# Two wide products in place of three for the first token block's attention scores

## The chip, the cores and the metric

The kernel runs on one core of one Trainium2 chip, as one launch. The metric is the device time in microseconds, from launch to end; the number given for a kernel is the median of its runs. All data are float32.

## What is computed

A trunk of two layers over 512 tokens of width 2048. Both layers shift and scale their input by a condition vector, mix it with an attention, multiply by a gate and normalise:

```
mod = silu(c) @ w_mod[l] + b_mod[l]; shift, scale, gate = split(mod, 3)
h = x * (1 + scale) + shift
y = attention_l(h)
x = layer_norm(sqrt(2) * x + gate * y)
```

Layer 0 is a differential attention with 8 heads. Each head has two pairs of queries and keys (component 0 and 1, width 128) and values of width 256. Layer 1 is a "forgetting" attention with 16 heads of width 128, whose keys and values come from a projection of layer 0's output. The reference goes through the queries in blocks of 128 tokens:

```
layer 0:  sc = q_block @ k.T * 128**-0.5 - slope * (t - s);  masked where s > t
          a = softmax(sc of component 0) - lam * softmax(sc of component 1);  o = a @ v
layer 1:  sc = q_block @ k.T * 128**-0.5 + F[t] - F[s];      masked where s > t
          o = softmax(sc) @ v
```

Only keys up to the query's own token count. So the first query block needs scores against 128 keys, the second against 256, the third against 384, the fourth against 512.

## The kernel before

**Products in two halves.** TensorE multiplies in a reduced float32 form (`F32R`). To keep float32 precision the kernel splits each operand into a high half (rounded to that form by ScalarE) and a low half (what is left, by VectorE), and forms three products instead of one: high by high, high by low, low by high. The function `products` (lines 199 to 203) issues them into one accumulating PSUM bank, and every large matrix product of the kernel goes through it or through its equivalent of the opening stage. In the rows of the profile the names of a product are those of the moving operand, then of the stationary one: `sc<-kbl,qh` moves the low half of the keys past the high half of the queries.

**Stages.** The opening stage builds the modulated input while the first weights arrive; its order on each engine is written out by hand in strings (`ORDER_PE` and others). Then comes a sequence of streamed groups (`group`): weights flow through a ring of staging tiles (`wst`), are split into `whi` and `wlo` (three buffers each, lines 106 and 107) and are multiplied with the activations, kept on chip in halves (`hh`, `hl`), into four banks called `acc`. A group is 32 bursts of six products.

**Attention between the bursts.** The attention of one head (layer 0) or of a pair of heads (layer 1) is cut into small steps kept in the list `pieces`. After every burst the function `tick` takes the next one from the list. So while the weights of the next projection stream through TensorE, the attention of the head before runs in between. At the end of a group `drain` empties the list before new queries and keys are written. After the opening stage the tile framework plans the order of the instructions on each engine from modelled times; it may part products that the code issues together.

**A score step.** `score` (line 859 and following in layer 0, line 1486 and following in layer 1) takes one of two PSUM banks (`sc`), forms the score of query block `i` against the `w = (i + 1) * 128` keys it may see, adds the bias (distance and mask, or forgetting sums and mask) with one VectorE instruction that also finds the row's extreme, and lets ScalarE take the exponential. Its width on TensorE is

```
n = max(w, 256)
```

so the first block is computed against 256 keys, and only the first 128 columns are read. After the scores of a block, the probabilities are turned by a VectorE transposition and two trips through DRAM (`turn`, `send`), split into halves (`take`: `ah`, `al` in layer 0, `pTh`, `pTl` in layer 1) and multiplied with the values (`values`, bank `o`). The last head of layer 0 and the last pair of layer 1 use TensorE's transposition instead.

**Where queries and keys are kept.** In layer 0, `evac_qk` (line 823) writes q0, q1, k0 and k1 of a head out of the accumulators as separate tiles of 128 x 512 for the high and low half (`q0h`, `q0l` and so on, one buffer each). In layer 1, `split_pair` (line 1472) does this for the keys of two heads (`kbh`, `kbl`, two buffers each).

Of the kernel before, what the change touches and what calls it, by code (L numbers as in the profile page):

```python
# [11 lines left out]
F32R = mybir.dt.float32r  # L12
I32 = mybir.dt.int32
AF = mybir.ActivationFunctionType
ALU = mybir.AluOpType

P = 128
D = 2048
KT = D // P
T = 512  # L20
# [117 lines left out]
def tile_yoco(  # L138
# [24 lines left out]
    V, S, PE, G = nc.vector, nc.scalar, nc.tensor, nc.gpsimd  # L163
# [3 lines left out]
    out = out[0]  # L167
# [31 lines left out]
    def products(dst, lhs, rhs, start, stop):  # L199

        PE.matmul(dst, lhs[0], rhs[0], start=start, stop=False)  # L201
        PE.matmul(dst, lhs[0], rhs[1], start=False, stop=False)  # L202
        PE.matmul(dst, lhs[1], rhs[0], start=False, stop=stop)  # L203


    ident = const.tile([P, P], F32, name="ident")
# [616 lines left out]
    def evac_qk(h):  # L823
        def fn(b, acc):
            name = ("q0", "q1", "k0", "k1")[b]
            hi = ap.tile([P, T], F32R, name=name + "h", tag=name + "h")
            lo = ap.tile([P, T], F32R, name=name + "l", tag=name + "l")
            if b < 2:
                S.activation(hi, acc, AF.Copy, scale=QS)
                V.scalar_tensor_tensor(lo, acc, QS, hi.bitcast(F32), op0=ALU.mult, op1=ALU.subtract)  # L830
            else:
                split(hi, lo, acc)
            cur[h, name] = (hi, lo)
        return fn

    def evac_vg(h):
# [16 lines left out]
    def attention_a(h, lead=3, late=(), spread=False):  # L853
# [5 lines left out]
        def score(i, comp):  # L859
            def fn():  # L860
                if i == 0 and comp == 0:
                    bias = ap.tile([P, 512], F32, name="bias", tag="bias", bufs=1)
                    V.scalar_tensor_tensor(bias, dist, -slope, mask, op0=ALU.mult, op1=ALU.add)
                    st["bias"] = bias
                if comp == 0:
                    st["mn", i] = ap.tile([P, 2], F32, name="mn", tag="mn", bufs=2)
                    st["rs", i] = ap.tile([P, 2], F32, name="rsum", tag="rsum", bufs=2)
                w = (i + 1) * P
                n = max(w, 256)
                q, k = cur[h, f"q{comp}"], cur[h, f"k{comp}"]  # L870
                sc = sc_bank()
                ts = slice(i * P, (i + 1) * P)
                products(sc[:, :n], (q[0][:, ts], q[1][:, ts]), (k[0][:, :n], k[1][:, :n]), True, True)
                e = ap.tile([P, 512], F32, name="e", tag="e", bufs=4)
                mn, rs = st["mn", i][:, comp : comp + 1], st["rs", i][:, comp : comp + 1]
                V.tensor_tensor_reduce(  # L876
                    out=e[:, :w], in0=sc[:, :w], in1=st["bias"][:, (3 - i) * P :], scale=-1.0, scalar=3.0e38,
                    op0=ALU.add, op1=ALU.min, accum_out=mn,
                )
                S.activation(e[:, :w], e[:, :w], AF.Exp, bias=mn, scale=-1.0, accum_out=rs)  # L880
                st["e", i, comp] = e
                if comp == 1:
                    r = st["rs", i]
                    V.reciprocal(r, r)
                    V.tensor_tensor(r[:, 1:2], r[:, 1:2], neglam, op=ALU.mult)
                    e0, e1 = st["e", i, 0], e
                    V.tensor_scalar(e0[:, :w], e0[:, :w], r[:, 0:1], None, op0=ALU.mult)
                    V.scalar_tensor_tensor(e0[:, :w], e1[:, :w], r[:, 1:2], e0[:, :w], op0=ALU.mult, op1=ALU.add)
            return fn
# [582 lines left out]
    def split_pair(p):  # L1472
        vh = bp.tile([P, TB, 256], F32R, name="vbh", tag="vbh", bufs=1)
        vl = bp.tile([P, TB, 256], F32R, name="vbl", tag="vbl", bufs=1)
        split(vh, vl, cur[p, "vld"])
        cur[p, "vB"] = (vh, vl)
        for hd in (2 * p, 2 * p + 1):
            kh = bp.tile([P, T], F32R, name="kbh", tag="kbh", bufs=2)
            kl = bp.tile([P, T], F32R, name="kbl", tag="kbl", bufs=2)
            split(kh, kl, KTs[hd])  # L1480
            cur[hd, "kB"] = (kh, kl)

    def attention_b(hd):
        st = {}

        def score(i):
            def fn():
                w = (i + 1) * P
                m = max(w, 256)
                q, k = cur[hd, "q"], cur[hd, "kB"]  # L1490
                sc = sc_bank()
                ts = slice(i * P, (i + 1) * P)
                products(sc[:, :m], (q[0][:, ts], q[1][:, ts]), (k[0][:, :m], k[1][:, :m]), True, True)
                bias = bp.tile([P, 512], F32, name="biasb", tag="biasb", bufs=2)
                V.scalar_tensor_tensor(
                    bias[:, :w], cur[hd, "nf"][:, :w], F[:, i, hd : hd + 1], mask[:, (3 - i) * P :], op0=ALU.add, op1=ALU.add
                )
                e = bp.tile([P, w], F32, name="eb", tag=f"eb{i}", bufs=1)
                mn = bp.tile([P, 1], F32, name="mnb", tag="mnb", bufs=3)
                rs = bp.tile([P, 1], F32, name="rsb", tag="rsb", bufs=3)  # L1500
                V.tensor_tensor_reduce(  # L1501
                    out=e[:, :w], in0=sc[:, :w], in1=bias[:, :w], scale=-1.0, scalar=3.0e38, op0=ALU.add, op1=ALU.min, accum_out=mn
                )
                S.activation(e[:, :w], e[:, :w], AF.Exp, bias=mn, scale=-1.0, accum_out=rs)  # L1504
                V.reciprocal(rs, rs)
                V.tensor_scalar(e[:, :w], e[:, :w], rs, None, op0=ALU.mult)
                st["e", i] = e
            return fn

        def turn(i):
            def fn():
                t = bp.tile([P, (i + 1) * P], F32, name="tb", tag=f"tb{i}", bufs=1)
                V.transpose(t.rearrange("p (b j c) -> p j b c", b=4, c=32), st["e", i].rearrange("p (j b c) -> p j b c", b=4, c=32))
                st["t", i] = dram.tile([P, (i + 1) * P], F32, name="turned", tag=f"turned{i}", bufs=2)
                nc.sync.dma_start(st["t", i], t)
            return fn

        def send(i):  # L1520
            def fn():
                src = st["t", i].rearrange("(a r) (b n) -> b r a n", a=4, b=4)
                to = pTl[:, 4 * i : 4 * i + 4, 0 : i + 1, :].bitcast(F32).rearrange("p a j c -> p a (j c)")
                for b in range(4):
                    nc.sync.dma_start(to[32 * b : 32 * b + 32], src[b])
            return fn

        def take(i):
            def fn():
                hi, lo = (t[:, 4 * i : 4 * i + 4, 0 : i + 1, :] for t in (pTh, pTl))  # L1530
                S.copy(hi, lo.bitcast(F32))
                V.tensor_tensor(lo, lo.bitcast(F32), hi.bitcast(F32), op=ALU.subtract)
            return fn

        def turn_at_once(i):
            def fn():
                pt = tr_bank()
                for j in range(i + 1):
                    PE.transpose(pt[:, j * P : (j + 1) * P], st["e", i][:, j * P : (j + 1) * P], ident)
                src = pt[:, : (i + 1) * P].rearrange("p (j a c) -> p a j c", a=4, c=32)  # L1540
                hi, lo = (t[:, 4 * i : 4 * i + 4, 0 : i + 1, :] for t in (pTh, pTl))
                S.copy(hi, src)
                V.tensor_tensor(lo, src, hi.bitcast(F32), op=ALU.subtract)
            return fn

        def values(j0, j1):
            def fn():
                if j0 == 0:
                    st["o"] = o_bank()
                vh, vl = cur[hd // 2, "vB"]  # L1550
                es = slice((hd % 2) * P, (hd % 2 + 1) * P)
                for j in range(j0, j1):
                    t0 = min(j * P, 256)
                    m0 = t0 // 32
                    o = st["o"][:, t0:].rearrange("p (m c) -> p m c", c=32)
                    products(o, (vh[:, j, es], vl[:, j, es]), (pTh[:, m0:, j, :], pTl[:, m0:, j, :]), j == 0, j == 3)
                if j1 == TB:
                    ogB[hd] = ktile("ogB")
                    V.scalar_tensor_tensor(ogB[hd], st["o"], 0.5, cur[hd, "sgT"], op0=ALU.mult, op1=ALU.mult)
            return fn  # L1560

        parts = (score, turn, send, take, turn_at_once)
        return *([part(i) for i in range(TB)] for part in parts), [values(0, 2), values(2, 4)]
# [135 lines left out]
```

## Time and profile before

| | |
|---|---|
| median of 3 runs | 1944.55 us (1944.41 to 1945.12) |
| profiled execution, first to last instruction (span) | 1943.2 us |
| mean granted TensorE clock | 0.998 |
| busy: TensorE, VectorE, ScalarE | 1922.5, 1351.3, 730.3 us |
| products on TensorE | 8973 |

No time of the profiled execution is listed apart from its span, so the span is set against the median of the runs: the median is 1.35 us longer. In the rows of the timeline the first number is the start in microseconds from the beginning of the span, the second the duration in microseconds, then come engine, line, operation, and output and operands by name; in brackets stands how long the engine sat idle before it and what ended that. In the grouped rows the numbers behind the first bar are the busy time of the group in microseconds and the mean duration of one in nanoseconds; behind the second bar is the engine's idle time before them, with what ended it. Products overlap: the duration of one is its latency, and the distance between two starts is what it takes from TensorE. Layer 0's attention lies between 200 and 830 us, layer 1's between 1389 and 1790 us.

### The profile page before, as it was taken

What the parts mean: (1) busy time and instruction counts of PE and PEld (TensorE: products, weight loads), DVE (VectorE), ACT (ScalarE), POOL (GpSimd) and SP (SyncE); (2) the same over time, 40 slices, a digit from 0 to 9 for tenths busy, and PEclk for the clock granted to TensorE, in tenths of its full rate; (3) what the DMA queues carried; (4) which work ended last, traced back from release to release, by engine and by line L of the source; (5) the groups of instructions that cost most, each with busy time, mean ns of one, the idle gap of its engine ahead of it and who ended that gap; (6) DMA issues with size and microseconds to landing.
All of it is one profiled execution on the core that took longest, in us unless ns stands there. A gap on an engine that the chain in (4) does not pass through costs nothing.

```text
span 1943.2 us, 25791 instructions
## 1 busy us (share of the span) xinstructions
PE 1922.5 (99%) x8973; PEld 1619.5 (83%) x8973; DVE 1351.3 (70%) x2514; ACT 730.3 (38%) x1250; POOL 2.2 (0%) x10
## 2 busy tenths in 40 slices
PE   8999999999999999999999999999999999999997
PEld 7888888888888888888889998888888888888886
DVE  6884588777676768567675657777566666677657
ACT  3546344323332334521273222224343434353123
POOL 0000000000000000000000000000000000000000
PEclk9999999999999999999999999999999999999999
DMA  9983466676767675377557756774355555554622
GB/s 339 383 300 115 151 187 201 210 230 188 239 192 225 202 237 167 121 241 225 171 174 256 266 187 214 251 260 158 118 154 148 153 155 154 152 171 153 222 91 105
DMA packets 351630, 382.19 MB, mean 197 GB/s; under 512 B 77926, under 2 KB 260860, under 8 KB 350732
## 3 DMA queue, kind: packets, MB, share of 16 engines
q1 hardware_dynamic: 348620, 376.35, 61.6%
q10 hardware_dynamic: 2880, 4.20, 0.6%
q8 instruction: 70, 1.15, 0.2%
q14 instruction: 60, 0.49, 0.1%
HBM read 348.65 MB, written 31.80 MB: 196 GB/s over the span
## 4 chain that ended last, share of the span: by engine, by line
PE 96%; DVE 3%; DMA 1%; issue 0%; ACT 0%; SPq 0%; DVEq 0%
PE acc L201 27%; PE acc L202 27%; PE acc L203 27%; PE acc L703 4%; PE sc L703 2%; PE o L201 1%; PE o L202 1%; PE o L203 1%; PE sc L203 1%; PE sc L202 1%; PE o L703 1%; PE sc L201 1%; DVE sacc L601 1%; PE tr L643 0%; PE tr L669 0%; PE tr L629 0%
## 5 line engine op out<-in xcount | busy, mean ns | idle before, releaser
L106 ACT CAST whi<-wst 128x1024 fp32r<-128x1024 f32 (+2 forms) x298 | 303.4, 1018 | 660.7 <-PE acc L203 353.2
L107 DVE TENSOR_TENSOR wlo<-wst,whi 128x1024 fp32r<-128x1024 f32 (+2 forms) x298 | 351.4, 1180 | 261.0 <-ACT whi L106 254.5
L201 PE MATMUL acc<-hh,whi 128*128 128x512 f32 x1184 | 463.5, 391 | 0.0
L202 PE MATMUL acc<-hl,whi 128*128 128x512 f32 x1184 | 461.8, 390 | 0.0
L203 PE MATMUL acc<-hh,wlo 128*128 128x512 f32 x1184 | 460.9, 390 | 0.0
L201 PE MATMUL acc<-whi,hh 128*128 128x512 f32 (+1 forms) x1168 | 444.4, 381 | 0.0
L202 PE MATMUL acc<-wlo,hh 128*128 128x512 f32 (+1 forms) x1168 | 442.3, 379 | 0.0
L203 PE MATMUL acc<-whi,hl 128*128 128x512 f32 (+1 forms) x1168 | 441.8, 378 | 0.0
L420 DVE SCALAR_TENSOR_TENSOR macc<-ms,cact,macc 128x512 f32<-128x512 f32 x307 | 229.1, 746 | 63.1 <-DMA ms<-in_w_mod_dram 41.1
L203 PEld LDWEIGHTS acc<-hh,wlo 128*128 128x128 f32 x1184 | 222.3, 188 | 47.6
L201 PEld LDWEIGHTS acc<-hh,whi 128*128 128x128 f32 x1184 | 222.5, 188 | 43.6 <-issue 0.6
L202 PEld LDWEIGHTS acc<-hl,whi 128*128 128x128 f32 x1184 | 222.4, 188 | 42.1
L203 PEld LDWEIGHTS acc<-whi,hl 128*128 128x128 f32 x1168 | 219.2, 188 | 36.5 <-DVE hl L1280 0.2
L201 PEld LDWEIGHTS acc<-whi,hh 128*128 128x128 f32 x1168 | 219.2, 188 | 34.8 <-DVE ztmp L1194 0.4
L202 PEld LDWEIGHTS acc<-wlo,hh 128*128 128x128 f32 x1168 | 219.3, 188 | 33.6 <-DVE wlo L107 0.3
L601 DVE SCALAR_TENSOR_TENSOR sacc<-sms,cact,sacc 128x512 f32<-128x512 f32 (+1 forms) x123 | 87.5, 712 | 5.9 <-DMA sms<-in_w_mod_dram 2.6
L880 ACT ACTIVATE e<-e,mn 128x128 f32<-128x128 f32 (+3 forms) x64 | 36.0, 563 | 113.5 <-DVE mn L876 99.6
L1504 ACT ACTIVATE eb<-eb,mnb 128x128 f32<-128x128 f32 (+1 forms) x64 | 36.0, 563 | 88.0 <-DVE mnb L1501 87.8
L876 DVE CUSTOM_DVE_ANT_0 e<-sc,bias 128x128 f32<-128x128 f32 (+3 forms) x64 | 31.0, 485 | 28.1 <-PE sc L203 27.8
L125 DVE TENSOR_TENSOR wlo<-wst,whi 128x768 fp32r<-128x768 f32 (+1 forms) x32 | 34.8, 1088 | 18.7 <-ACT whi L118 9.9
L703 PE MATMUL acc<-whi,hh 128*128 128x512 f32 x128 | 46.4, 394 | 0.0
L703 PE MATMUL acc<-whi,hl 128*128 128x512 f32 x128 | 45.9, 394 | 0.0
(285 smaller groups left out, 1999.0 us busy)
## 6 DMA issues: line engine op xcount, KB each, us to landing
wst<-in_a_w_in_dram SPq DMA_DIRECT2D x240, 256.0 KB, 4.1
ms<-in_w_mod_dram SPq DMA_DIRECT2D x136, 256.0 KB, 3.7
ms<-in_kv_w_mod_dram SPq DMA_DIRECT2D x64, 512.0 KB, 4.0
wst<-in_b_w_in_dram SPq DMA_DIRECT2D x128, 256.0 KB, 3.0
sms<-in_w_mod_dram SPq DMA_DIRECT2D x56, 512.0 KB, 7.7
wst<-in_kv_w_dram SPq DMA_DIRECT2D x40, 512.0 KB, 4.2
ms<-in_w_mod_dram SPq DMA_DIRECT2D x32, 512.0 KB, 4.5
wst<-in_a_w_out_dram SPq DMA_DIRECT2D x32, 512.0 KB, 4.4
```

Of the source, the lines that this page charges most:

```text
L106: self.nc.scalar.copy(hi[:, :, :w], st[:, :, :w])
L107: self.nc.vector.tensor_tensor(lo[:, :, :w], st[:, :, :w], hi[:, :, :w].bitcast(F32), op=ALU.subtract)
L125: self.nc.vector.tensor_tensor(lo[:, :, :w], st[:, :, :w], hi[:, :, :w].bitcast(F32), op=ALU.subtract)
L201: PE.matmul(dst, lhs[0], rhs[0], start=start, stop=False)
L202: PE.matmul(dst, lhs[0], rhs[1], start=False, stop=False)
L203: PE.matmul(dst, lhs[1], rhs[0], start=False, stop=stop)
L420: ins = V.scalar_tensor_tensor(acc, w, cact[:, kt : kt + 1], acc, op0=ALU.mult, op1=ALU.add)
L601: V.scalar_tensor_tensor(acc, w, sc, acc, op0=ALU.mult, op1=ALU.add)
L703: PE.matmul(bank[n, bk], l, r, start=start, stop=stop, skip_group_check=True)
L876: V.tensor_tensor_reduce(out=e[:, :w], in0=sc[:, :w], in1=st["bias"][:, (3 - i) * P :], scale=-1.0, scalar=3.0e38, op0=ALU.add, op1=ALU.mi ...
L880: S.activation(e[:, :w], e[:, :w], AF.Exp, bias=mn, scale=-1.0, accum_out=rs)
L1504: S.activation(e[:, :w], e[:, :w], AF.Exp, bias=mn, scale=-1.0, accum_out=rs)
```

## The change

High and low halves of a query or key are placed in one tile, `[P, 2, T]`. For the first query block (`i == 0`) of both layers, the score no longer goes through `products`. The new function `corner` takes the first 128 columns of the high keys and the first 128 of the low keys as one moving operand of 2 x 128 columns, and multiplies it once with the high and once with the low half of the queries. The bank then holds, in columns 0 to 127, the products with the high keys, and in columns 128 to 255 those with the low keys (the product low by low is among them now). VectorE adds the two halves: in layer 0 the second half plus the bias is written to the unused part of the tile `e` and takes the place of the bias; in layer 1 the second half is added into the bias tile. The other three query blocks are as before.

```diff
+    def corner(sc, q, k):
+        dst, both = (t[:, :, 0:P] for t in (sc[:, 0 : 2 * P].rearrange("p (u n) -> p u n", u=2), k))
+        PE.matmul(dst, q[0], both, start=True, stop=False)
+        PE.matmul(dst, q[1], both, start=False, stop=True)
...
     def evac_qk(h):
-            hi = ap.tile([P, T], F32R, name=name + "h", tag=name + "h")
-            lo = ap.tile([P, T], F32R, name=name + "l", tag=name + "l")
+            both = ap.tile([P, 2, T], F32R, name=name, tag=name)
+            hi, lo = both[:, 0, :], both[:, 1, :]
...
+            cur[h, name, "both"] = both
...
     score, layer 0:
-                products(sc[:, :n], (q[0][:, ts], q[1][:, ts]), (k[0][:, :n], k[1][:, :n]), True, True)
+                bias = st["bias"][:, (3 - i) * P :]
+                if i:
+                    products(sc[:, :n], (q[0][:, ts], q[1][:, ts]), (k[0][:, :n], k[1][:, :n]), True, True)
+                else:
+                    corner(sc, (q[0][:, ts], q[1][:, ts]), cur[h, f"k{comp}", "both"])
+                    V.tensor_tensor(e[:, P : 2 * P], sc[:, P : 2 * P], bias, op=ALU.add)
+                    bias = e[:, P : 2 * P]
                 V.tensor_tensor_reduce(
-                    out=e[:, :w], in0=sc[:, :w], in1=st["bias"][:, (3 - i) * P :], scale=-1.0, scalar=3.0e38,
+                    out=e[:, :w], in0=sc[:, :w], in1=bias, scale=-1.0, scalar=3.0e38,
...
     split_pair, layer 1:
-            kh = bp.tile([P, T], F32R, name="kbh", tag="kbh", bufs=2)
-            kl = bp.tile([P, T], F32R, name="kbl", tag="kbl", bufs=2)
+            both = cur[hd, "kboth"] = bp.tile([P, 2, T], F32R, name="kb", tag="kb", bufs=2)
+            kh, kl = both[:, 0, :], both[:, 1, :]
...
     score, layer 1:
-                products(sc[:, :m], (q[0][:, ts], q[1][:, ts]), (k[0][:, :m], k[1][:, :m]), True, True)
+                if i:
+                    products(sc[:, :m], (q[0][:, ts], q[1][:, ts]), (k[0][:, :m], k[1][:, :m]), True, True)
+                else:
+                    corner(sc, (q[0][:, ts], q[1][:, ts]), cur[hd, "kboth"])
                 bias = ...
+                if i == 0:
+                    V.tensor_tensor(bias[:, :w], sc[:, P : 2 * P], bias[:, :w], op=ALU.add)
```

## The prediction

> **What bounds the kernel now.** I read the page first: its header, the busy times, the chain that ended last.
>
> ```profile
> span 1943.2 us, 25791 instructions
> ...
> PE 1922.5 (99%) x8973; PEld 1619.5 (83%) x8973; DVE 1351.3 (70%) x2514; ACT 730.3 (38%) x1250; POOL 2.2 (0%) x10
> ...
> PE 96%; DVE 3%; DMA 1%; issue 0%; ACT 0%; SPq 0%; DVEq 0%
> ```
>
> TensorE is busy for 1922.5 of 1943.2 us and carries 96% of the chain. A busy PE could still be a PE that waits, so the second view is the list of PE's waits; its longest entry and the only one that concerns an attention step:
>
> ```profile
> PE tr L228 <- DMA crow<-in_c_dram: 2.5, 1, 2.5
> PE o L202 <- DVE pTl L1532: 0.5, 1, 0.5
> ```
>
> The first lies at the very start. No score product (L201 to L203 into sc) is in the list with a VectorE or ScalarE wait, and no weight half. So in both attention stages a TensorE product that disappears shortens the span by its whole slot, and VectorE work is free until it makes a product late. The third view is the timeline around one first-block score of the second layer (PE alone):
>
> ```profile
> 1389.02 0.39 PE L203 MATMUL acc<-hh,wlo 128*128 128x512 f32 x1
> 1389.25 0.28 PE L201 MATMUL sc<-kbh,qh 128*128 128x256 f32 x1
> 1389.36 0.28 PE L202 MATMUL sc<-kbl,qh 128*128 128x256 f32 x1
> 1389.48 0.28 PE L203 MATMUL sc<-kbh,ql 128*128 128x256 f32 x1
> 1389.60 0.40 PE L201 MATMUL acc<-hh,whi 128*128 128x512 f32 x1
> ```
>
> The second column, 0.28 us, is the latency of a product; what it costs is the distance from its start to the next start. A product of 512 columns takes 0.23, one of 256 takes 0.11 to 0.12, and the three together 0.35 us.
>
> **The change part by part: the products.** How many scores are touched is read from the VectorE groups, shapes apart, once in the window of the first layer's attention and once in that of the second's. A first-block score is the one whose biased sum is 128 columns wide:
>
> ```profile
> L876 DVE CUSTOM_DVE_ANT_0 e<-sc,bias 128x128 f32<-128x128 f32 x16 | 4.6, 288 | 10.0 <-PE sc L203 10.0
> ```
> ```profile
> L1532 DVE TENSOR_TENSOR pTl<-pTl,pTh 128x128 fp32r<-128x128 f32 x15 | 4.4, 291 | 0.9 <-ACT pTh L1531 0.9
> L1501 DVE CUSTOM_DVE_ANT_0 eb<-sc,biasb 128x128 f32<-128x128 f32 x16 | 4.4, 272 | 6.3 <-PE sc L203 6.3
> ```
>
> 16 in the first layer (8 heads, 2 components) and 16 in the second (16 heads): 32. Each loses one product of 256 columns and its weight load. The two that stay still have 256 moving columns and still take 256 output columns, so by the rows above a corner goes from 0.35 to 0.23 or 0.24 us. The removed slot is 0.115 to 0.125 us, and 32 of them are 3.7 to 4.0 us; I take 3.8.
>
> What the trace of before does not show for a score is a moving operand in two stretches of 128 columns that lie 512 elements apart. The nearest rows are the value products of the second layer over the last two key blocks: their moving operand is cut into eight stretches of 32 columns (the tile pTh, indexed by row group and key block), which is more broken than the new one. Of six such products the first and the last:
>
> ```profile
> 1435.38 0.28 PE L201 MATMUL o<-pTh,vbh 128*128 128x256 f32 x1
> ...
> 1435.99 0.28 PE L203 MATMUL o<-pTh,vbl 128*128 128x256 f32 x1
> ```
>
> Five distances make 0.61 us, 0.122 each: no slower than the score's own by more than a few ns. The other bounds come from the spacings: a product of 512 columns costs 0.23 and two of 256 cost 0.24, so a fresh start is worth about 0.01 us. If each stretch counted as a start, a new product would cost 0.13, a corner 0.26, and the saving would be 0.09 x 32 = 2.9 us. At the other end it could be 0.11 as for the first of the three, a saving of 0.13 x 32 = 4.2 us. I take 3.8 by the value rows and keep 2.9 to 4.2. The Trainium skill has a price for this too: by its page "TensorE: Matmul & The Clock Gate", section "Back-to-back issue gap", a product of 256 columns follows the last after 256/2.4 + 2.5 = 109 ns, and by that estimate 32 slots would give 3.5 us; the rows here stand at 0.11 to 0.12, and the row decides.
>
> **VectorE's additions.** Every corner gains one addition of 128 columns, with one operand in PSUM. The three group rows above bracket it: 272 to 291 ns, whether the operand comes from sc or from SBUF; I take 0.29 us, 32 x 0.29 = 9.3 us of VectorE, of which it has 1943.2 - 1351.3 = 592 us idle. Queued behind it on VectorE are the reduction of the same score, then what follows there (reciprocals, transposes, the low halves of weights); ScalarE's exponential waits for the reduction. In the first layer the reduction sat waiting for TensorE for 10.0 us in all over its 16 corners, in the second 6.3 us, so there is room at the place itself. Two users of the result are on TensorE. One is the transposition of the last head of the first layer, which is close behind its score:
>
> ```profile
> 800.49 0.35 DVE L888 SCALAR_TENSOR_TENSOR e<-e,rsum 128x128 f32<-128x128 f32 x1
> ```
> ```profile
> 803.71 0.27 PE L897 MATMUL tr<-ident,e 128*128 128x128 f32 x1
> ```
>
> The tile is there at 800.84 and is read at 803.71: 2.9 us cover two additions of 0.29. The other is the value product of the second layer, which waits for the last split (pTl) of the first head of a pair while VectorE handles the second head's corner. An ordinary pair:
>
> ```profile
> 1401.71 0.25 DVE L1501 CUSTOM_DVE_ANT_0 eb<-sc,biasb 128x128 f32<-128x128 f32 x1
> ...
> 1404.42 0.42 DVE L1501 CUSTOM_DVE_ANT_0 eb<-sc,biasb 128x256 f32<-128x256 f32 x1 [0.45 <-PE sc L203]
> ...
> 1411.74 1.22 DVE L107 TENSOR_TENSOR wlo<-wst,whi 128x1024 fp32r<-128x1024 f32 x1
> ...
> 1414.55 0.40 PE L201 MATMUL o<-pTh,vbh 128*128 128x512 f32 x1
> 1414.69 0.65 DVE L1532 TENSOR_TENSOR pTl<-pTl,pTh 128x512 fp32r<-128x512 f32 x1
> 1414.79 0.39 PE L202 MATMUL acc<-hl,whi 128*128 128x512 f32 x1
> ...
> 1415.48 0.42 PE L202 MATMUL o<-pTl,vbh 128*128 128x512 f32 x1
> ```
>
> pTl ends at 1415.34 and is used at 1415.48: only 0.14 us to spare. But between the corner at 1401.71 and pTl, VectorE idles for 0.45 us on a product of TensorE, whose time does not move with VectorE, and that alone swallows 0.29. Cost: nothing. In the last streamed group it is different, as VectorE also splits the gated outputs (hl) there:
>
> ```profile
> 1710.70 0.16 DVE L1505 RECIPROCAL rsb<-rsb 128x1 f32<-128x1 f32 x1 [0.62 <-ACT eb L1504]
> ...
> 1712.51 0.25 DVE L1501 CUSTOM_DVE_ANT_0 eb<-sc,biasb 128x128 f32<-128x128 f32 x1
> ...
> 1720.01 0.16 DVE L1505 RECIPROCAL rsb<-rsb 128x1 f32<-128x1 f32 x1 [0.17 <-ACT eb L1504]
> ...
> 1726.36 0.65 DVE L1532 TENSOR_TENSOR pTl<-pTl,pTh 128x512 fp32r<-128x512 f32 x1
> ...
> 1727.06 0.19 PEld L202 LDWEIGHTS o<-pTl,vbh 128*128 128x128 f32 x1 [0.95 <-DVE pTl L1532]
> ```
>
> From the corner at 1712.51 to pTl the only idle time is 0.17 us, and it waits for an exponential that VectorE itself feeds, so it moves along. TensorE already waits there, and the addition makes it wait longer: 0.2 us (additions overlap their neighbours by some 0.08) to 0.29. I charge 0.25, once.
>
> **The joined tiles** (high and low half of q, k in one buffer) change no instruction's size. The first corner product now needs the low half of k, which it needed 0.11 us later before; PE's waits name no such half, so nothing. A buffer is now given back when the readers of both halves are done, 0.12 us apart; the pieces of a head are drained before its buffers are written anew, so nothing either. No DMA is added or moved.
>
> **Sum.** -3.8 + 0.25 = -3.55 us on the span of 1943.2, that is 1939.65. The median of the runs shown is 1944.55, 1.35 above that span; the same distance gives 1941.0. A measurement of this kernel can tell about 0.2%, 3.9 us, from no change: the line is at 1940.66, and the sum ends 0.3 us short of it.
>
> **The rivals.** *Placement for the better, 0.22.* The order on each engine after the opening stage is planned from modelled times, as the ordinary pair shows: the code issues the three o products together, and the trace has three acc products between the first and the second. A later VectorE in the plan can move the product of 1727.06 behind further acc products. Its weights waited 0.95 us where a slot is 0.23, so about 0.7 us would come back and the 0.25 not fall due: 3.8 + 0.7 = 4.5, 1940.05; with the upper bound of the slot 1939.65. For it: the corner's additions stand before exactly that product. Against: plans shift either way.
>
> *Placement for the worse, 0.13, on the other side.* In an ordinary pair the value product has 0.14 us to spare. If the plan puts one more low half of weights (1.22 us, the row at 1411.74) between the last idle stretch and pTl, the product waits 1.22 + 0.29 - 0.14 = 1.37 us, in each of 7 pairs: 9.6 us, less 3.8, gives 1950.4. It decides from three pairs on (4.1 us eats the gain), and passes the 0.2% line above at six (8.2 - 3.8 = 4.4). Against: the additions alone are 0.29 against 0.45 us of idle time.
>
> *No gain, 0.05.* A weight load lasts 0.19 us (the row at 1727.06), longer than a slot of 0.12. Should the two stretches keep the next load from overlapping, two products would cost 0.35 as three did, and the time stays at 1944.5. The value products with eight stretches, at 0.122, speak against it.
>
> **How the numbers follow.** The forecast has 0.60. Its own spread is the slot's bounds: 1940.6 to 1941.9. About a third of it, 0.21, lies beyond the 0.2% line (a slot of 0.13, or the 0.25 not falling due), and 0.39 within. Faster: 0.21 + 0.22 = 0.43. Within 0.2%: 0.39 + 0.05 = 0.44. Slower: 0.13. The range holds the forecast and the better placement, from 1939.3 (0.3 under that rival's best) to 1942.3 (0.4 over the forecast's worst, for some small waits of VectorE's making), and leaves out the two others, 0.18.
>
> **What would show it.** PE's count falls by 32 to 8941, VectorE's rises by 32. In the timeline a first-block score is two products of 256 columns, 0.23 to 0.24 us from its first start to the next acc product: 0.26 would mean that stretches cost, 0.35 that nothing was won. The added row of VectorE is 128x128 at 0.27 to 0.29 us, x16 in each layer. PE's waits still hold one o product on pTl, near 0.75 us instead of 0.5; if it is gone the better placement came, and if there are several, or a wait on wlo, the worse one. The prediction is wrong if the gain in the two attention windows is not about 1.9 us each.

## The result, and the profile after

| | before | changed |
|---|---|---|
| median | 1944.54 us (16 runs) | 1940.84 us (16 runs) |
| ratio | | 0.9981, 95% interval 0.9974 to 0.9987 |
| profiled execution: time, span | span 1943.2 us | 1940.17 us, span 1938.4 us |

The kernel became 3.70 us faster, 0.19%. The forecast was 3.55 us (1941.0).

The page of the changed kernel, the lines that answer to those of before:

```profile
span 1938.4 us, 25779 instructions
PE 1918.7 (99%) x8941; PEld 1616.2 (83%) x8941; DVE 1358.4 (70%) x2546; ACT 731.4 (38%) x1250; POOL 2.2 (0%) x10
```

TensorE has 32 products fewer (8941), VectorE 32 instructions more (2546). TensorE is still busy for 99% of the span. The spans differ by 4.8 us, more than the medians do, in part because the profiled execution of the changed kernel was one of its quickest; below, stretches inside the span are compared, which do not contain the opening stage.

The timeline of TensorE around the first corner of layer 1, the answer to the six rows of the prediction:

```profile
1386.40 0.39 PE L203 MATMUL acc<-hh,wlo 128*128 128x512 f32 x1
1386.62 0.28 PE L208 MATMUL sc<-kb,qh 128*128 128x256 f32 x1
1386.74 0.28 PE L209 MATMUL sc<-kb,ql 128*128 128x256 f32 x1
1386.86 0.40 PE L201 MATMUL acc<-hh,whi 128*128 128x512 f32 x1
```

Two products, 1386.62 to 1386.86: 0.24 us (0.232 before rounding), where three took 0.35. Their moving operand in two stretches starts the next product after 0.12 us, exactly as the contiguous one did. All 32 corners look like this one.

To see where the rest lies, the span is cut at scores, in each kernel at the start of the first product: layer 0's stretch runs from the first score of all to the last score of block 1 of the last head, layer 1's is cut the same way. The ends of layer 0's stretch, before and changed (the last score is still three products, block 1 being untouched):

```profile
220.13 0.28 PE L201 MATMUL sc<-k0h,q0h 128*128 128x256 f32 x1
801.97 0.28 PE L201 MATMUL sc<-k1h,q1h 128*128 128x256 f32 x1
```
```profile
219.51 0.28 PE L208 MATMUL sc<-k,q 128*128 128x256 f32 x1
799.35 0.28 PE L201 MATMUL sc<-k,q 128*128 128x256 f32 x1
```

581.83 became 579.84 us, and with layer 1 read the same way:

| us | opening, to the first score | layer 0 stretch | between | layer 1 stretch |
|---|---|---|---|---|
| before | 220.13 | 581.83 | 587.28 | 376.89 |
| changed | 219.51 | 579.84 | 587.27 | 374.69 |
| difference | -0.62 | -1.99 | -0.01 | -2.20 |

Sixteen corners at 0.120 us are 1.92 us. Layer 0 gives 0.07 more than that, layer 1 gives 0.28 more. The opening stage is untouched by the change and varies from run to run (219.5 to 220.6 us in the kernels below).

TensorE's waits behind the opening stage, of the changed kernel (the first lies at 987 us, between the two attention stages):

```profile
PE sc L1299 <- ACT n L1274: 0.4, 1, 0.4
PE o L201 <- ACT ah L943: 0.2, 1, 0.2
```

The 0.5 us for pTl is gone from the list. That was not the forecast, which had it grow.

How well a stretch repeats can be read from kernels whose instructions stand in the same order on TensorE, VectorE and ScalarE inside it. In layer 0 these are the changed kernel and two of the experiments below (layer 0 alone, and the second place): 579.84, 580.04 and 579.80 us. In layer 1 they are the kernel before, the joined tiles alone and layer 0 alone, 376.89, 376.48 and 376.77; and the changed kernel and layer 1 alone, 374.69 and 374.75. One pair differs more, by 1.35 us; it is named at the joined tiles.

### The profile page after: what moved, and what is told of

Same layout as the page of the kernel before. It is cut to its first block, busy times and chain, and to the rows that moved or that the text cites. A ratio compares the mean times of both kernels' runs of the same rounds, so it can differ in the third digit from the quotient of the medians.

```text
span 1938.4 us, 25779 instructions
## 1 busy us (share of the span) xinstructions
PE 1918.7 (99%) x8941; PEld 1616.2 (83%) x8941; DVE 1358.4 (70%) x2546; ACT 731.4 (38%) x1250; POOL 2.2 (0%) x10
## 4 chain that ended last, share of the span: by engine, by line
PE 80%; DVE 2%; DMA 0%; issue 0%; ACT 0%; DVEq 0%
PE acc L201 25%; PE acc L202 25%; PE acc L203 25%; PE o L201 1%; PE o L202 1%; PE o L203 1%; PE sc L203 1%; PE sc L202 1%; PE sc L201 1%; DMA wst<-in_kv_w_dram 0%; DVE wlo L107 0%; PE sc L1299 0%; DVE ztmp L1207 0%; PE sc L209 0%; PE sc L208 0%
## 5 line engine op out<-in xcount | busy, mean ns | idle before, releaser
L889 DVE CUSTOM_DVE_ANT_0 e<-sc,bias 128x256 f32<-128x256 f32 (+2 forms) x48 | 26.4, 551 | 27.0 <-PE sc L203 26.9
```

The costliest lines, as they stand in the source:

```text
L889: V.tensor_tensor_reduce(out=e[:, :w], in0=sc[:, :w], in1=bias, scale=-1.0, scalar=3.0e38, op0=ALU.add, op1=ALU.min, accum_out=mn,)
```

## The experiments

Two theories stood against each other. *Slots*: the gain is the slot of the product that went, 0.120 us at each of 32 corners, and the additions are hidden. *Additions and planning*: VectorE's 9 us come through in part, or the gain (or a large share of it) is an accident of a new order on the engines. Stretches are from the profile of each kernel, medians from 7 to 11 runs with the runs of before beside them.

**The change without the additions.**

```diff
-                    V.tensor_tensor(e[:, P : 2 * P], sc[:, P : 2 * P], bias, op=ALU.add)
-                    bias = e[:, P : 2 * P]
...
-                if i == 0:
-                    V.tensor_tensor(bias[:, :w], sc[:, P : 2 * P], bias[:, :w], op=ALU.add)
```

> The changed kernel without its 32 VectorE additions (the second halves of the sums are left out, so the first block's scores lack the low keys). My theory, slots: a corner is worth the TensorE slot of the product that went, 32 x 0.120 = 3.84 us, and the additions are covered. Then this takes the time of the changed kernel, 1940.8 us within 0.5; the layer 0 stretch (first score product to the last score product of block 1 of the last head) is 2.0 us shorter than before's 581.84, the layer 1 stretch (first to last such product) 1.9 to 2.3 shorter than before's 376.88. Rival, additions: VectorE's 9.3 us come through in part; then this kernel is faster than the changed one by 1 us or more, and both stretches shrink by over 2.5 us.

1941.72 us, ratio 0.9983 (0.9974 to 0.9992); layer 0 stretch 579.75, layer 1 stretch 374.46. Without the additions the stretches are 0.09 and 0.23 us shorter than the changed kernel's, so 32 additions show with some 0.3 us together, which is within what the runs below show single waits to move. The median is not better than the changed kernel's but 0.9 higher, outside the 0.5 us expected: outside the attention stages, between the two stretches, 588.71 us in place of 587.27. Its list of TensorE's waits names the place, a transposition of layer 0's output:

```profile
PE sc L1297 <- DVE n L1310: 1.2, 1, 1.2
PE sc L1297 <- ACT n L1272: 0.5, 1, 0.5
```

The first of these lines is in neither before nor the changed kernel. Nothing of the edit touches that place, and between the two stretches the order of the instructions on TensorE, VectorE and ScalarE, and that in which transfers are issued, is the same in both kernels. What differs is when a transfer to DRAM landed, for which VectorE's copy waits, here and in the changed kernel:

```profile
994.79 1.29 DVE L1310 COPY n<-sc 128x512 f32<-128x512 f32 x2 [1.43 <-DMA n_dram<-n]
```
```profile
993.19 1.29 DVE L1312 COPY n<-sc 128x512 f32<-128x512 f32 x2 [0.15 <-DMA n_dram<-n]
```

Why it landed later stays open. The wait on pTl in the last streamed group is gone here as well, in another way than in the changed kernel (see below).

**Three products, with the additions.**

```diff
-                    corner(sc, (q[0][:, ts], q[1][:, ts]), cur[h, f"k{comp}", "both"])
-                    V.tensor_tensor(e[:, P : 2 * P], sc[:, P : 2 * P], bias, op=ALU.add)
-                    bias = e[:, P : 2 * P]
+                    products(sc[:, :n], ...)                          # as for the other blocks
+                    V.tensor_tensor(e[:, P : 2 * P], sc[:, P : 2 * P], bias, op=ALU.add)
```

(and the same in layer 1)

> Three products as before, joined tiles, and the 32 additions issued with a result that nobody reads (the chain of VectorE has them, TensorE keeps its products). Slots: the time of before, 1944.5 us within 0.5, stretches 581.8 and 376.9 within 0.4. Additions: slower than before by 1 us or more. If the vanished wait of the last streamed group (a value product on pTl, 0.7 us in before) comes from planning with the additions, it is gone here too, and the layer 1 stretch is 376.2 to 376.5.

1945.35 us, ratio 1.0003 (0.9994 to 1.0011); stretches 582.18 and 376.58. The median is 0.8 us above before's, more than the 0.5 us expected, but the interval of the ratio holds 1. Stretches are 0.35 longer and 0.31 shorter than before's, within the 0.4 us expected: in the attention stages the additions alone cost nothing that shows.

**The joined tiles alone.**

> High and low halves in one tile, three products, no additions. Slots: no change, 1944.5 us within 0.5, stretches 581.84 and 376.88 within 0.1, and the value product of the last streamed group waits for pTl as in before (0.7 us). Rival, buffers: if giving back a tile later or sooner were part of the gain, it is faster than before by over 0.5 us, or the wait is gone here.

1944.97 us, ratio 1.0001 (0.9992 to 1.001); stretches 582.93 and 376.48. The time is that of before, but the expectation of stretches within 0.1 us failed: layer 0 is 1.1 us longer, layer 1 is 0.4 shorter. For layer 0 the list of waits has a line that before has not:

```profile
PE acc L201 <- DVE sg L855: 1.1, 1, 1.1
```

One product of a projection waits for a gate tile, and VectorE, which writes that tile, had idled just before for a transfer of weights:

```profile
414.38 0.75 DVE L426 SCALAR_TENSOR_TENSOR macc<-ms,cact,macc 128x512 f32<-128x512 f32 x1 [1.46 <-DMA ms<-in_w_mod_dram]
```

The kernel with layer 1's corners alone (next) has the same order in layer 0 on all three engines and in the issue of transfers, and neither idle time is there: its stretch is 581.58, 1.35 us shorter. So this wait is no matter of the planned order. In layer 1 the 0.4 us are in the main the wait on pTl, which is 0.2 us here where it was 0.7 before (from the starts of the products around it), with the order of before.

**One layer at a time.**

> The change in layer 0 alone (16 corners), layer 1 with three products and no additions. Slots: half the gain, 16 x 0.12 = 1.9 us, 1942.6 within 0.5; layer 0 stretch 579.84, layer 1 stretch 376.88 with the wait of before. Rival, additions or planning: the two layers' shares are unequal, 1 us or less (or 3 us or more) in layer 0.

> The change in layer 1 alone, layer 0 with three products and no additions (joined tiles in both). Slots: 16 x 0.12 = 1.9 us, 1942.6 within 0.6; layer 1 stretch 374.9 within 0.3, layer 0 stretch between 582.0 and 583.2 (before and joined tiles). Together with the run of layer 0 alone the two gains add up to that of the changed kernel within 0.8 us. If planning and not slots were the larger part, the sum misses by more.

Layer 0 alone: 1942.87 us, ratio 0.999 (0.9981 to 0.9999), stretches 580.04 and 376.77. Layer 1 alone: 1942.74 us, ratio 0.9991 (0.9982 to 1.0), stretches 581.58 and 374.75. Each stretch shrinks where its corners are changed, by 1.79 and 2.14 us, and the other stays within 0.25 of before's (for layer 1 alone this is 0.4 below the expected band, which leaned on the joined tiles). By the medians the two gains are 1.69 and 1.90, together 3.59, against 3.70 for the whole change. Each median carries an interval of about 1.7 us to either side, as large as the gain itself, so it is the stretches that show the slots to add up; this is the clearest evidence for them.

**Three products of 128 columns in place of the change.** Could the unneeded second half simply be left away?

```diff
-                n = max(w, 256)
+                n = w
-                m = max(w, 256)
+                m = w
```

> The kernel before with the first block's three products on its own 128 keys only (no second half, no joined tiles, no additions). From the slots of before (512 columns 0.23, 256 columns 0.12 us) a straight line gives about 0.065 us for 128 columns, three 0.20 in place of 0.35: 32 x 0.155 = 5 us faster than before, 1939.6, and better than the changed kernel. Second theory, floor: a product has a least slot near that of 256 columns (its weight load lasts 0.19 us), then three take 0.35 and nothing is won, 1944.5. Third, narrow streams run slower per column: the transpositions by TensorE, 128 columns wide, start 0.11 us apart, three would take 0.33, 1943.8; above 0.12 each it is slower than before.

1943.37 us, ratio 0.9994 (0.9985 to 1.0003). The timeline of the first narrow score, products first, then the weight loads of one in layer 1 (each product's load comes before it):

```profile
219.77 0.22 PE L201 MATMUL sc<-k0h,q0h 128*128 128x128 f32 x1
219.83 0.28 PE L202 MATMUL sc<-k0l,q0h 128*128 128x128 f32 x1
219.94 0.27 PE L203 MATMUL sc<-k0h,q0l 128*128 128x128 f32 x1
220.06 0.44 PE L201 MATMUL acc<-hh,whi 128*128 128x512 f32 x1
220.34 0.40 PE L202 MATMUL acc<-hl,whi 128*128 128x512 f32 x1
```
```profile
1388.87 0.19 PEld L202 LDWEIGHTS sc<-kbl,qh 128*128 128x128 f32 x1
...
1388.98 0.19 PEld L203 LDWEIGHTS sc<-kbh,ql 128*128 128x128 f32 x1
...
1389.09 0.19 PEld L201 LDWEIGHTS acc<-hh,whi 128*128 128x128 f32 x1
...
1389.20 0.19 PEld L202 LDWEIGHTS acc<-hl,whi 128*128 128x128 f32 x1
```

The first narrow product takes 0.06 us, as a straight line from the wide ones says. The second and third take 0.11 to 0.12, and the weight loads before them start no closer than 0.11 us one behind the other; and the product of 512 columns behind them takes 0.28 instead of 0.23, since its own load and the next one were held up. From the first start to 220.34 it is 0.57 us, against 0.585 over the same five starts before. The floor theory was right in kind: in a row of products with a weight load each, a product takes at least about 0.11 us, the spacing of the loads. A product of 256 columns (0.12) just fills it, and this is why two wide products win where three narrow ones do not. The third theory's figure, 0.33 for three, is met as well, if the 0.05 us of the product behind is counted; but the first narrow product with its 0.06 us speaks against a stream that is slow in itself. By the Trainium skill, page "TensorE: Matmul & The Clock Gate", section "LDWEIGHTS (loading the stationary operand)", a load lasts its columns divided by 1.2 in ns, 107 ns for 128 columns; the distance of 0.11 us agrees, while the rows show each load as lasting 0.19. The interval of the ratio holds 1, and what the median undercuts before by (1.3 us) is mostly not the scores: layer 0's stretch, with 16 narrow corners, is 581.75 against 581.83. Layer 1's, 375.07 against 376.89, shrank by more than its 16 corners explain (about 0.25 us). Most of the rest lies at the value products, in another planned order: the 42 of 512 columns take 10.07 us in place of 10.75, and the wait on pTl in the last streamed group falls from 0.7 to 0.3 us.

**The additions five times.**

```diff
+                    for _ in range(4):
+                        V.tensor_tensor(e[:, 2 * P : 3 * P], sc[:, P : 2 * P], bias, op=ALU.add)
```

(and the same in layer 1)

> The changed kernel with four more additions of 128 columns behind each corner's own (their results are read by nobody), 1.2 us more of VectorE per corner, 37 us in all. It asks how far the cover reaches. Cover theory: in layer 0 VectorE has idle time at each score (10 us over 16 corners before), so the layer 0 stretch stays within 0.5 us of the changed kernel's 580.07; in layer 1 the value product of a pair's first head has 0.1 to 0.2 us to spare behind idle stretches of 1.7 us, so 1.2 us is mostly swallowed in an ordinary pair and the layer 1 stretch grows by 0 to 2.5 us from 374.93, with waits of value products on pTl in the list; total 1941 to 1944. Rival, VectorE nearly free of slack: 0.5 us or more per corner comes through, total above 1957; or below: no change at all within 0.3 us.

1942.31 us, ratio 0.9988 (0.9979 to 0.9997): 128 more additions, which lengthen VectorE's busy time by 21.8 us (1380.2 against the changed kernel's 1358.4; neighbours overlap), for 1.5 us of time. Stretches 582.54 and 373.63. The layers answered the other way round than expected. Layer 1 became 1.1 us shorter than the changed kernel's, as its value products no longer wait for pTl (the 42 of 512 columns take 9.99 us in place of 10.97). Layer 0 grew by 2.7 us: 1.0 us at its 210 value products, 1.1 us in one wait. That wait on TensorE in the timeline, its line in the list of waits, and VectorE just before:

```profile
333.25 0.39 PE L203 MATMUL acc<-hh,wlo 128*128 128x512 f32 x1
334.62 0.36 PE L201 MATMUL sc<-k,q 128*128 128x256 f32 x1 [0.98 <-DVE mn L891]
```
```profile
PE sc L201 <- DVE mn L891: 1.0, 1, 1.0
```
```profile
331.92 0.75 DVE L426 SCALAR_TENSOR_TENSOR macc<-ms,cact,macc 128x512 f32<-128x512 f32 x1 [1.58 <-DMA ms<-in_w_mod_dram]
```

The score of block 1 waits for the reduction that reads its PSUM bank: there are two banks, and the five additions of the corner two scores earlier keep one of them in use. A product that took 0.23 took 1.37. But the additions alone did not do it. The plan spread them between other instructions, and one of these idled 1.58 us for a transfer, in the midst of the five; without that, by an estimate from these rows, the reduction (done at 334.46) would have ended 0.6 us before the score needed the bank. So VectorE's work at a corner becomes a cost not through the total of its busy time, but where the bank isn't free two scores later.

**The same trick at a second place.** In layer 1 the values of the last key block meet 256 query columns, of which only the last 128 are not zero. Two wide products into a bank of their own take the place of three:

```diff
-    pTh = bp.tile([P, 16, TB, 32], F32R, name="pTh")
-    pTl = bp.tile([P, 16, TB, 32], F32R, name="pTl")
+    pT = bp.tile([P, 2, 16, TB, 32], F32R, name="pT")
+    pTh, pTl = pT[:, 0], pT[:, 1]
...
+                    PE.matmul(dst, vh[:, 3, es], pT[:, :, 12:16, 3, :], start=True, stop=False)
+                    PE.matmul(dst, vl[:, 3, es], pT[:, :, 12:16, 3, :], start=False, stop=True)
+                    V.tensor_copy(last, vc[:, 0:P])
+                    V.tensor_tensor(last, vc[:, P : 2 * P], last, op=ALU.add)
+                    V.tensor_tensor(last, st["o"][:, 3 * P :], last, op=ALU.add)
```

(the product with the gate is cut in two, at column 384)

> The changed kernel, and the same trick where layer 1 multiplies probabilities with values of the last key block: only the last 128 of the 256 query columns are not zero there. High and low probabilities in one tile, two products of 2 x 128 columns into a bank of their own, not three of 256; VectorE copies and adds the halves (three more small instructions and one instruction cut in two, about 1 us per head, 16 us). Slots: 16 x 0.12 = 1.9 us less than the changed kernel, 1938.9 within 0.8, layer 1 stretch 373.0 within 0.7 (it varied by about 1 us between kernels with other plans). Rival, additions: VectorE's 16 us show and nothing is won, 1940.5 or more.

1939.15 us, ratio 0.9971 (0.9961 to 0.9982), the fastest of all; the layer 1 stretch is 372.76, 1.93 us less than the changed kernel's. Only 14 of the 16 new places lie inside the stretch, as it ends before the values of the last pair, so slots make 14 x 0.12 = 1.68 of it, and the rest is in other waits. By the medians all 16 gained 1.69, where slots make 1.92. Its TensorE timeline at the place:

```profile
1414.80 0.28 PE L203 MATMUL o<-pT,vbl 128*128 128x256 f32 x1
1414.92 0.28 PE L1578 MATMUL vc<-pT,vbh 128*128 128x256 f32 x1
1415.04 0.28 PE L1579 MATMUL vc<-pT,vbl 128*128 128x256 f32 x1
1415.16 0.40 PE L201 MATMUL acc<-hh,whi 128*128 128x512 f32 x1
```

Eight stretches of 32 columns, high and low from two regions of the tile, and still 0.12 us each.

## Why the prediction was right

**The slot: right.** Taken at 3.8 us, it is 32 x 0.120 = 3.84 us, seen at each corner and confirmed by the runs of one layer at a time. **The moving operand in two stretches: right**; of the bounds 2.9 to 4.2 the value rows pointed to the correct one. The 109 ns per slot of the Trainium skill ("TensorE: Matmul & The Clock Gate", section "Back-to-back issue gap", which gives the formula for an isolated product) would have given 3.5 us; the trace does not agree, with 0.12.

**The additions: right in price, and in cover but for the value products below.** The groups of the changed kernel:

```profile
L887 DVE TENSOR_TENSOR e<-sc,bias 128x128 f32<-128x128 f32 x16 | 4.6, 286 | 8.2 <-PE sc L209 8.2
```
```profile
L1515 DVE TENSOR_TENSOR biasb<-sc,biasb 128x128 f32<-128x128 f32 x16 | 4.4, 273 | 5.5 <-PE sc L209 5.5
```

286 and 273 ns, where 290 was assumed, and VectorE still waits 8.2 and 5.5 us for TensorE in front of them.

**The 0.25 us in the last streamed group: wrong, and so is its sign.** This step reasoned that every instruction from the corner to pTl would keep its order on VectorE and come 0.2 to 0.29 us later. VectorE and TensorE around that pTl in the changed kernel:

```profile
1717.30 0.68 DVE L1519 CUSTOM_DVE_ANT_0 eb<-sc,biasb 128x512 f32<-128x512 f32 x1
...
1719.05 0.55 DVE L1550 TENSOR_TENSOR pTl<-pTl,pTh 128x384 fp32r<-128x384 f32 x1
...
1721.93 0.65 DVE L1550 TENSOR_TENSOR pTl<-pTl,pTh 128x512 fp32r<-128x512 f32 x1
```
```profile
1722.14 0.40 PE L201 MATMUL o<-pTh,vbh 128*128 128x512 f32 x1
...
1722.83 0.40 PE L202 MATMUL o<-pTl,vbh 128*128 128x512 f32 x1
```

pTl ends at 1722.58, before its product wants it at 1722.83: no wait. To compare the two kernels, both are measured from the first product of the last score before, which started here in the kernel before and in the changed one:

```profile
1720.24 0.39 PE L201 MATMUL sc<-kbh,qh 128*128 128x512 f32 x1
1725.68 0.40 PE L201 MATMUL o<-pTh,vbh 128*128 128x512 f32 x1
```
```profile
1716.24 0.39 PE L201 MATMUL sc<-kb,qh 128*128 128x512 f32 x1
```

The last pTl started 6.12 us behind it before and 5.69 us in the changed kernel. The first value product came 5.44 us behind it before, 24 products on, and now comes 5.90 us behind it, 26 products on: two more acc products stand ahead of it. Together that is 0.9 us, more than the wait. So the rival "placement for the better" came true at its place, and by its own mechanism. Its price was about 0.7 us; measured, the acc product ahead had a slot of 0.92 us where 0.23 is usual, and the pTl product one of 0.34 in place of 0.24, 0.8 us in all.

The experiments say which part of the edit moved the value product. It is still 24 products on with the joined tiles alone, with layer 0's corners alone and without the additions (22 with narrow products). It is 26 on with layer 1's corners alone, 29 with three products and additions, 31 with the additions five times. The additions put it later, as the rival had it. The earlier pTl is less clearly the edit's: with the order of before it comes between 5.65 us (joined tiles) and 6.12 (before), and the wait is 0.2 to 0.7 us. Without the additions it comes after 5.24 us, which ends the wait without any move.

Part of the 0.8 us was paid back. In ordinary pairs, where the prediction saw no cost, the value product now stands so close behind pTl that its weights wait:

```profile
1413.02 0.19 PEld L202 LDWEIGHTS o<-pTl,vbh 128*128 128x128 f32 x1 [0.22 <-DVE pTl L1550]
```

The product itself loses 0.03 us there, in six pairs, 0.2 in all; the first value product of the head after the last pTl above (at 1740.71) loses 0.1, and acc products lose 0.2. Net, layer 1 stands 0.28 us beyond its slots.

**The sum.** -3.84 from slots, -0.35 from other waits in the two stretches (-1.99 - 2.20 + 3.84), nothing in between, against the -3.8 and +0.25 of the prediction. The medians (-3.70) contain the opening stage, whose variation from run to run is as large as that difference. So the slots carry the forecast, and that the median lies within 0.2 us of it is partly luck: the term for the last streamed group had the wrong sign, 1.0 us off at its place (+0.25 forecast, -0.8 measured), and the waits elsewhere, which the prediction put at nothing, made up for some of it. The measured time lies within 0.2% of before by a hair, as the sum had it.

## What to carry to other kernels

Where a multiplication in high and low halves needs only 128 columns, put both halves side by side as one moving operand: two products of 256 columns cost 0.24 us, three of 128 cost nearly what three of 256 do, because weight loads start 0.11 us apart anyway. Cost a VectorE addition not by its busy time but by the buffer it keeps occupied: with two PSUM banks, one addition per score was all but free, and five held a bank too long once, when a transfer came late between them. And single waits of about 1 us come and go at places that an edit doesn't touch, partly since the order is planned anew, partly in the very same order, behind a transfer that lands later. So before a wait is put down to the plan, compare the order on each engine; and read an effect of a few us from the slots in a stretch, with one part undone at a time, and not from one median.

## What the runs showed of the hardware

Products of 128 columns: 0.06 us for the first behind a wide product, 0.11 to 0.12 us for those that follow it with a weight load each, and 0.05 us more for the wide product behind them. A moving operand of 2 x 128 or 2 x 4 x 32 columns is as fast as 256 in one piece (0.12 us).
